# Loading a matmul's first B chunks in column halves and A by row tile, with two pairs of matmuls kept back behind each second transpose

## Chip, cores, metric

One core of one Trainium2 chip. The metric is device microseconds of the whole launch.

Besides the device time each run gives the span, from the core's first to its last instruction. I call the difference **the time outside the span**. Differences here are tenths of a microsecond in 1783, so I give the runs' spread and look for the same thing in the traces. The means of five runs are good to about 0.1 us. Kernels are compared only within the same rounds.

## The reference

```python
# a: 4096 x 4096, b: 4096 x 4096, float32; alpha = 0.01
x = np.matmul(a, b)
return np.where(x > 0, x, alpha * x)
```

## The kernel before

The output is computed in regions of 512 rows by 1024 columns: eight PSUM banks of 128 x 512, for row tile `mt` 0 to 3 and column half `nt` 0 or 1. Inputs are rounded to bf16. From the second stage on, loads round on the way, and VectorE transposes A. The first stage (1024 of K, in eight chunks) is hand-made to get TensorE (PE) going early: float32 loads on SyncE's queue, rounding on VectorE and ScalarE, and transposes of A on PE with an identity. A's part comes in two runs of 512 of K, for B's chunks 0 to 3 and 4 to 7. All is issued in one order list:

```python
order = [("b", 0), ("a", 0, 0, 1), ("a", 1, 0, 1), ("a", 2, 0, 1), ("a", 3, 0, 1)]
order += [("b", 1), ("b", 2), ("a", 0, 1, 2), ("b", 3), ("a", 2, 1, 1), ("a", 3, 1, 1)]
order += [("b", c) for c in range(4, KC)]
# ("b", chunk)   ("a", first tile, run of 512 of K, number of tiles)
for what, i, *more in order:
    if what == "a":
        ...
        nc.sync.dma_start(a_in[:, i:i + tiles, k], src)
    elif i:                                   # chunk 0 comes on ScalarE's queue
        nc.sync.dma_start(b_in[i], b_rows(pairs[0], 0, i))       # 512 KB
...
def turn_a(i, r, tiles):
    ...                                       # 4 PE transposes a tile, into bank ps7 for run 1
    if r and not shared:                      # tiles 0 and 1 of run 1: the copy out is held
        leaving.append(lambda: nc.vector.tensor_copy(to, turned))
    elif r:
        nc.vector.tensor_copy(to, turned)     # tiles 2 and 3
    else:
        nc.scalar.copy(to, turned)

def round_b(i):
    for nt, copy in ((0, nc.scalar.copy), (1, nc.vector.tensor_copy)):
        copy(b0[:, i, columns(nt)], b_in[i][:, columns(nt)])
    for leave in leaving:                     # the held copy follows the next chunk's cast
        leave()
    leaving.clear()
...
def work(keep=0):                             # emit all ready (mt, chunk) pairs but the last keep
    now = waiting[:len(waiting) - keep]
    ...
```

Bank `ps7` serves the transposes and is also the accumulator of tile 3's right half, the **late bank**. That accumulator can start only when the second copy out of the transposes is done.

## Time and profile before

| | before |
|---|---|
| device time, median of the first six runs | 1783.43 us (1783.37 to 1783.80) |
| span of the trace | 1781.684 us |
| time outside the span | 1.79 us |
| PE's first matmul of chunk 1 | 9.73 us |
| PE restarts with the late bank, the **restart** | 16.11 us |
| last matmul starts | 1778.289 us |
| transfers on SyncE's input queue / built instructions of VectorE | 14 / 311 |

The page and the timeline are in the prediction. The way to read them: PE is busy 99% of the span, so the only question is where its few idle tenths lie. They lie before the restart. After it PE has work without a break, save 0.15 us.

### The profile page before, as it was taken

The numbers are of one execution on the slowest core, as the hardware profiler recorded it, in microseconds if no ns is written. First come the engines' busy times: TensorE is split into PE (matmuls) and PEld (weight loads), VectorE is DVE, ScalarE is ACT, GpSimd is POOL, SyncE is SP. The second block draws the span as 40 slices with busy tenths as digits, with TensorE's granted clock in tenths as the row PEclk, the third lists the DMA queues.
The fourth block names the chain that finished last, engine by engine and source line by source line (L and its number), as shares of the span: only waits on it lengthen the run. The fifth ranks groups of instructions, "written<-read, shape, count | busy, mean of one in ns | idle before, by whom it ended". The sixth has DMA issues, their size and how long they took to land.

```text
span 1781.7 us, 18049 instructions
## 1 busy us (share of the span) xinstructions
PE 1767.0 (99%) x8104; PEld 807.7 (45%) x8267; DVE 144.8 (8%) x123; ACT 152.5 (9%) x271; POOL 365.8 (21%) x667
## 2 busy tenths in 40 slices
PE   9999999999999999999999999999999999999999
PEld 4444444444444444444444444444444444444444
DVE  4530000032000000002200000000220000000000
ACT  2010000000000000000000000000000000000001
POOL 5630200433002020144201202014320110301000
PEclk9999999999999999999999999999999999999999
DMA  9995653987039174398704917449860481835511
GB/s 249 201 253 114 117 129 87 190 131 124 36 95 189 48 121 116 95 191 134 124 24 96 187 48 143 93 104 196 134 121 13 112 172 48 164 73 120 117 48 47
DMA packets 161548, 214.06 MB, mean 120 GB/s; under 512 B 41536, under 2 KB 90816, under 8 KB 161472
## 3 DMA queue, kind: packets, MB, share of 16 engines
q0 software_dynamic: 140608, 139.50, 49.2%
q10 hardware_dynamic: 18432, 67.12, 9.7%
q1 hardware_dynamic: 2432, 6.29, 0.9%
q8 instruction: 64, 1.05, 0.2%
q14 instruction: 12, 0.10, 0.0%
HBM read 285.21 MB, written 67.11 MB: 198 GB/s over the span
## 4 chain that ended last, share of the span: by engine, by line
PE 98%; DMA 1%; issue 1%; POOL 0%; ACT 0%; DVE 0%
PE ps L160 98%; DMA bt<-in_b_dram 1%; DMA b_in<-in_b_dram 1%; POOL bt L140 0%; DVE at L300 0%; ACT bt L306 0%; PE turned L291 0%; ACT o L453 0%
## 5 line engine op out<-in xcount | busy, mean ns | idle before, releaser
L160 PE MATMUL ps<-bt,at 128*128 128x512 bf16 x8061 | 1761.1, 378 | 9.6 <-DVE at L300 0.6
L160 PEld LDWEIGHTS <-at 128*128 128x128 bf16 x8224 | 804.2, 98 | 964.3 <-issue 1.8
L140 POOL DMA_DIRECT2D bt<-in_b_dram x408 | 217.2, 539 | 1085.9 <-PE ps L160 963.7
L438 ACT ACTIVATE o<-ps 128x512 f32<-128x512 f32 x239 | 130.2, 595 | 1518.1 <-PE ps L160 1443.3
L123 DVE STREAM_TRANSPOSE at<-a 128x1024 uint32<-128x1024 uint32 (+2 forms) x64 | 112.5, 1791 | 1153.7 <-DMA a<-in_a_dram 595.8
L117 POOL DMA_DIRECT2D a<-in_a_dram x252 | 147.9, 593 | 194.3 <-DVE at L123 132.6
L238 DVE TENSOR_TENSOR part<-ps,part 128x512 f32<-128x512 f32 x32 | 20.2, 685 | 25.6 <-PE ps L160 25.6
L241 ACT ACTIVATE o<-part 128x1024 f32<-128x1024 f32 x8 | 8.5, 1057 | 77.1 <-DVE part L238 64.6
L306 ACT CAST bt<-b_in 128x512 bf16<-128x512 f32 x8 | 4.9, 618 | 9.7 <-DMA b_in<-in_b_dram 9.7
L234 DVE COPY part<-ps 128x512 f32<-128x512 f32 x8 | 5.3, 681 | 4.2 <-PE ps L160 4.2
L236 ACT COPY part<-ps 128x512 f32<-128x512 f32 x8 | 4.4, 593 | 13.7 <-issue 8.1
L89 PE MATMUL wp<-w 128*128 128x512 bf16 x11 | 4.3, 569 | 1.2 <-DVE x L80 1.2
L306 DVE CAST bt<-b_in 128x512 bf16<-128x512 f32 x8 | 3.4, 425 | 4.7 <-DMA b_in<-in_b_dram 4.7
L291 PE MATMUL turned<-ident,a_rounded 128*128 128x128 bf16 x32 | 3.0, 222 | 0.7 <-DVE a_rounded L274 0.7
L274 DVE CAST a_rounded<-a_in 128x512 bf16<-128x512 f32 (+1 forms) x7 | 3.2, 468 | 5.7 <-DMA a_in<-in_a_dram 5.6
L291 PEld LDWEIGHTS <-a_rounded 128*128 128x128 bf16 x32 | 2.3, 114 | 2.7 <-DVE a_rounded L274 2.1
L89 PEld LDWEIGHTS <-w 128*128 128x128 bf16 x11 | 1.4, 136 | 3.6 <-issue 2.4
L359 POOL CAST x<-bt 128x1 f32<-128x1 bf16 x1 | 0.2, 183 | 12.1 <-ACT bt L306 12.1
L302 ACT COPY at<-turned 128x512 bf16<-128x512 bf16 x4 | 2.3, 586 | 0.7 <-PE turned L291 0.5
L86 ACT ACT_TABLE_LOAD x1 | 1.3, 1283 | 1.2 <-PEq L472 1.2
L453 ACT ACTIVATE o<-ps 128x256 f32<-128x256 f32 x2 | 0.8, 383 | 6.0 <-PE ps L160 6.0
L300 DVE COPY at<-turned 128x1024 bf16<-128x1024 bf16 x1 | 0.7, 692 | 0.8 <-PE turned L291 0.8
(10 smaller groups left out, 2.1 us busy)
## 6 DMA issues: line engine op xcount, KB each, us to landing
bt<-in_b_dram POOLq DMA_DIRECT2D x408, 256.0 KB, 7.8
out_dram<-o ACTq DMA_DIRECT2D x127, 512.0 KB, 3.1
a<-in_a_dram POOLq DMA_DIRECT2D x244, 128.0 KB, 5.2
b_in<-in_b_dram SPq DMA_DIRECT2D x7, 512.0 KB, 8.5
a_in<-in_a_dram SPq DMA_DIRECT2D x6, 256.0 KB, 5.2
b_in<-in_b_dram ACTq DMA_DIRECT2D x1, 512.0 KB, 4.7
a_in<-in_a_dram SPq DMA_DIRECT2D x1, 512.0 KB, 7.5
a<-in_a_dram POOLq DMA_DIRECT2D x8, 64.0 KB, 5.6
```

The lines of the kernel that those rows point to most:

```text
L89: nc.tensor.matmul(wp, w[:, :P], w, start=True, stop=True)
L117: nc.gpsimd.dma_start(to, src.rearrange("(g i) w -> i g w", i=32))
L123: nc.vector.transpose(dst.rearrange("p c m e -> p c (m e)").bitcast(U32) .rearrange("p c (g i) -> p g c i", i=32), held[0][:, 4 * t0:4 * t ...
L140: nc.gpsimd.dma_start(new_b(pi, u)[:, c, :], b_rows(n, u, c))
L160: nc.tensor.matmul(ps, plain(t)[:, c, rows] if (mb, h, u) == (0, 0, 0) else t[:, c // 2, rows, c % 2], bt[pi, u][:, c, cols or slice(nt * ...
L234: nc.vector.tensor_copy(kept, banks[mt, nt])
L236: nc.scalar.copy(kept, banks[mt, nt])
L238: nc.vector.tensor_add(kept, banks[mt, nt], kept)
L241: nc.scalar.activation(o, part[h][:, mt, :], LRELU, alpha=alpha)
L291: nc.tensor.transpose(turned[:, c, slot, :], cols[:, i + t, c, :], ident)
L306: copy(b0[:, i, columns(nt)], b_in[i][:, columns(nt)])
L438: nc.scalar.activation(o[:, cols], banks[mt, nt], LRELU, alpha=alpha)
```

## The change

The intent: left halves of a chunk can be rounded before right ones have landed; A's second run can be transposed tile by tile; and more ready matmuls stand behind each second transpose, to cover the copy out. The core of the diff (renamings left out):

```diff
-    order += [("b", 1), ("b", 2), ("a", 0, 1, 2), ("b", 3), ("a", 2, 1, 1), ("a", 3, 1, 1)]
+    order += [("b", 1), ("b", 2), ("a", 0, 1), ("a", 1, 1), ("b", 3), ("a", 2, 1), ("a", 3, 1)]
...
-            nc.sync.dma_start(b_in[i], b_rows(pairs[0], 0, i))
+            for nt in range(NP):
+                nc.sync.dma_start(b_in[i][:, columns(nt)], b_rows(pairs[0], 0, i)[:, columns(nt)])
...
-        if r and not shared:
-            leaving.append(lambda: nc.vector.tensor_copy(to, turned))
-        elif r:
-            nc.vector.tensor_copy(to, turned)
-        else:
-            nc.scalar.copy(to, turned)
+        if slot == tiles - 1:
+            copy = nc.vector.tensor_copy if r else nc.scalar.copy
+            copy(to, turned[r].rearrange("p c t m -> p c (t m)"))
...
-        return next(m for m in range(len(order) - n) if order[n + 1 + m][0] == "b")
+        return next(m for m in range(KC) if order[n + 1 + m][0] == "b" or not order[n + 1 + m][2])
...
-            work(ahead(n) if r else 0)
+            work(ahead(n) + 1 if r and ahead(n) else 0)
...
-                work(max(1, ahead(n)))
+                work(ahead(n) + 1)
```

More of the change, by code (lines that the diff above doesn't have):

```diff
@@ L250 @@
     a_in = bt_pool.tile([P, MT, KW], FP32, name="a_in", tag="bt")
-    order = [("b", 0), ("a", 0, 0, 1), ("a", 1, 0, 1), ("a", 2, 0, 1), ("a", 3, 0, 1)]
-    order += [("b", 1), ("b", 2), ("a", 0, 1, 2), ("b", 3), ("a", 2, 1, 1), ("a", 3, 1, 1)]
+    order = [("b", 0), ("a", 0, 0), ("a", 1, 0), ("a", 2, 0), ("a", 3, 0)]
+    order += [("b", 1), ("b", 2), ("a", 0, 1), ("a", 1, 1), ("b", 3), ("a", 2, 1), ("a", 3, 1)]
     order += [("b", c) for c in range(4, KC)]
@@ L256, in columns, with run @@
         return slice(nt * NT, (nt + 1) * NT)
+    def run(r):
+        return slice(r * rw, (r + 1) * rw)
     for what, i, *more in order:
         if what == "a":
-            r, tiles = more
-            k = slice(r * rw, (r + 1) * rw)
-            src = a[i * P:(i + tiles) * P, k].rearrange("(t p) k -> p t k", p=P)
-            nc.sync.dma_start(a_in[:, i:i + tiles, k], src)
+            r = more[0]
+            nc.sync.dma_start(a_in[:, i, run(r)], a[i * P:(i + 1) * P, run(r)])
         elif i:
-            nc.sync.dma_start(b_in[i], b_rows(pairs[0], 0, i))
+            for nt in range(NP):
+                nc.sync.dma_start(b_in[i][:, columns(nt)], b_rows(pairs[0], 0, i)[:, columns(nt)])
@@ L266 @@
     a0 = new_a(0, 0, 0)
     b0 = new_b(0, 0)
-    leaving = []
-    both = []
-    def round_a(i, r, tiles):
-        k = slice(r * rw, (r + 1) * rw)
-        nc.vector.tensor_copy(a_rounded[:, i:i + tiles, k], a_in[:, i:i + tiles, k])
-    def turn_a(i, r, tiles):
-        k = slice(r * rw, (r + 1) * rw)
-        shared = r and tiles == 1
-        if shared and i == MT - 1:
-            turned = both.pop()
-        else:
-            tag = "ps7" if r else f"ps{4 + i}"
-            turned = psum_pool.tile([P, per, 2 if r else 1, P], BF16, name="turned", tag=tag)
-        if shared and i < MT - 1:
-            both.append(turned)
-        cols = a_rounded[:, :, k].rearrange("m t (p c) -> m t c p", c=per)
-        for t in range(tiles):
-            slot = i - (MT - 2) if shared else t
-            for c in range(per):
-                nc.tensor.transpose(turned[:, c, slot, :], cols[:, i + t, c, :], ident)
-        if both:
-            return
-        first = MT - 2 if shared else i
-        to = plain(a0)[:, r * per:(r + 1) * per, first * P:(i + tiles) * P]
-        turned = turned.rearrange("p c t m -> p c (t m)")
-        if r and not shared:
-            leaving.append(lambda: nc.vector.tensor_copy(to, turned))
-        elif r:
-            nc.vector.tensor_copy(to, turned)
-        else:
-            nc.scalar.copy(to, turned)
@@ new lines, with round_a, turn_a @@
+    turned = {}
+    def round_a(i, r):
+        nc.vector.tensor_copy(a_rounded[:, i, run(r)], a_in[:, i, run(r)])
+    def turn_a(i, r):
+        tiles = 2 if r else 1
+        slot = i % tiles
+        if slot == 0:
+            tag = "ps7" if r else f"ps{4 + i}"
+            turned[r] = psum_pool.tile([P, per, tiles, P], BF16, name="turned", tag=tag)
+        cols = a_rounded[:, i, run(r)].rearrange("m (p c) -> m c p", c=per)
+        for c in range(per):
+            nc.tensor.transpose(turned[r][:, c, slot, :], cols[:, c, :], ident)
+        if slot == tiles - 1:
+            to = plain(a0)[:, r * per:(r + 1) * per, (i - slot) * P:(i + 1) * P]
+            copy = nc.vector.tensor_copy if r else nc.scalar.copy
+            copy(to, turned[r].rearrange("p c t m -> p c (t m)"))
@@ L306, in round_b @@
             copy(b0[:, i, columns(nt)], b_in[i][:, columns(nt)])
-        for leave in leaving:
-            leave()
-        leaving.clear()
     there = {"a": [], "b": []}
@@ L342 @@
         if what == "a":
-            r, tiles = more
+            r = more[0]
             if n > 1:
-                round_a(i, r, tiles)
-            turn_a(i, r, tiles)
-            work(ahead(n) if r else 0)
-            there["a"] += [(i + t, r) for t in range(tiles)]
-            waiting += [(i + t, c) for t in range(tiles) for c in there["b"] if c // per == r]
+                round_a(i, r)
+            turn_a(i, r)
+            work(ahead(n) + 1 if r and ahead(n) else 0)
+            there["a"].append((i, r))
+            waiting += [(i, c) for c in there["b"] if c // per == r]
         else:
```

## The prediction

> **What bounds the kernel now.** I read the page first, then the PE timeline of the first 25 us, then the other engines' timeline there, then the chain of waits.
>
> ```profile
> span 1781.7 us, 18049 instructions
> ...
> PE 1767.0 (99%) x8104; PEld 807.7 (45%) x8267; DVE 144.8 (8%) x123; ACT 152.5 (9%) x271; POOL 365.8 (21%) x667
> ...
> L160 PE MATMUL ps<-bt,at 128*128 128x512 bf16 x8061 | 1761.1, 378 | 9.6 <-DVE at L300 0.6
> ```
>
> TensorE is the bound. In the trace single 128x512 matmuls start 0.2157 us apart; 8192 of them are worth 1767.0 us, the busy time on the page (the 378 ns is a pipelined latency, and 131 records are missing). So 99% of the span is work that the change does not touch. Going through the starts of all PE records, I find after 16.11 us one gap that is no missing record: 0.15 us at 23.9, where the second region's first bank waits for its copy out. Everything to be won lies before 16.11 us. The PE timeline there (start, length with the last one's latency, count, idle time before):
>
> ```profile
> 8.40 0.60 PE L160 MATMUL ps<-bt,at 128*128 128x512 bf16 x2
> 9.22 3.48 PE L160 MATMUL ps<-bt,at 128*128 128x512 bf16 x14 [0.22 <-ACT at L302]
> 12.54 0.61 PE L291 MATMUL turned<-ident,a_rounded 128*128 128x128 bf16 x8
> 13.35 1.02 PE L160 MATMUL ps<-bt,at 128*128 128x512 bf16 x4 [0.20 <-ACT bt L306]
> 14.26 0.41 PE L291 MATMUL turned<-ident,a_rounded 128*128 128x128 bf16 x4
> 14.51 0.59 PE L160 MATMUL ps<-bt,at 128*128 128x512 bf16 x2
> 14.95 0.39 PE L291 MATMUL turned<-ident,a_rounded 128*128 128x128 bf16 x4
> 15.17 0.38 PE L160 MATMUL ps<-bt,at 128*128 128x512 bf16 x1
> 16.11 9.16 PE L160 MATMUL ps<-bt,at 128*128 128x512 bf16 x40 [0.57 <-DVE at L300]
> ```
>
> I count idle in issue slots, since the shown idle subtracts a latency: 0.2157 for a matmul, 0.056 for a transpose. Before 11.2 us there are waits that the change leaves alone. From the eight transposes on there are three: for the cast of B chunk 3 about 0.15 us (12.98 plus one unrecorded matmul is 13.20; it goes on at 13.35), for the cast of A tile 2 (14.21 to 14.26 and a 0.03 slower first transpose) 0.08, and for the copy out of the last transpose, 15.17+0.216=15.384 to 16.113, 0.73. Sum 0.96 us. The copy matters because the late accumulator (row tile 3, right half) lives in the bank that the transposes use.
>
> The others in that stretch (L306 casts B, L274 casts A, L298 and L300 copy transposes out):
>
> ```profile
> 10.04 0.43 DVE L306 CAST bt<-b_in 128x512 bf16<-128x512 f32 x1 [0.87 <-DMA b_in<-in_b_dram]
> 11.47 0.69 DVE L274 CAST a_rounded<-a_in 128x1024 bf16<-128x1024 f32 x1 [0.99 <-DMA a_in<-in_a_dram]
> 12.67 0.62 ACT L306 CAST bt<-b_in 128x512 bf16<-128x512 f32 x1 [2.01 <-DMA b_in<-in_b_dram]
> 12.68 0.43 DVE L306 CAST bt<-b_in 128x512 bf16<-128x512 f32 x1 [0.52 <-DMA b_in<-in_b_dram]
> 13.18 0.69 DVE L298 COPY at<-turned 128x1024 bf16<-128x1024 bf16 x1
> 13.79 0.79 DVE L274 CAST a_rounded<-a_in 128x512 bf16<-128x512 f32 x2
> 15.37 0.69 DVE L300 COPY at<-turned 128x1024 bf16<-128x1024 bf16 x1 [0.79 <-PE turned L291]
> ```
>
> Before, VectorE casts chunk 3 first and copies transposes after. The chain of waits names the same pieces:
>
> ```profile
> 5.49 7.16 DMA b_in<-in_b_dram
> ...
> 12.67 0.63 ACT bt L306
> ...
> 15.37 0.70 DVE at L300
> ...
> 16.11 7.50 PE ps L160 x34
> ```
>
> [...] the casts of B on ScalarE and VectorE wait behind earlier copies that are not ready. My result hangs on this order. [...] Halves have rows of 2 KB where whole chunks have 4 KB. The trace gives a 2 KB packet 85 to 88 ns and a 4 KB one 159 to 167, so the finer form costs some 5%. [...] chunk 7 took 1.83 us (17.84 to 19.67) against 1.28 of its neighbours, once the software queue's packets had begun at 17.57.
>
> **The change part by part.** The order of both built programs shows: the same 64 matmuls and 32 transposes in the first part, the same from the late bank on; the last chunks alone come in another size.
>
> *Halves.* Landings before: A tiles 5.29, 6.12, 6.79, 7.45, chunks 1 and 2 8.72 and 10.02, A's second run 11.37, chunk 3 12.65, last two A tiles 13.33 and 13.99. A 256 KB piece of 2 KB rows takes 0.667 (the A tiles: 0.67, 0.66, 0.68, 0.66). From 7.45 on the pieces land at 8.12, 8.79 (chunk 1), 9.45, 10.12 (chunk 2), 10.79, 11.45 (A 0, 1), 12.12, 12.79 (chunk 3), 13.45, 14.12 (A 2, 3). Left halves come 0.55 earlier, all else 0.1 later. Chunk 1's left half gains nothing: ScalarE is at its copies until 9.06.
>
> *Second run by tile.* The casts become 10.81 to 11.24 and 11.48 to 11.90, 0.43 each: ready before PE wants them.
>
> *Order.* PE is unchanged up to 11.24. Then two matmuls (11.24, 11.456), four transposes 11.67 to 11.895, two matmuls, four transposes 12.33 to 12.55, three matmuls, chunk 3's left one: no wait until 13.41. But there is a new order on VectorE: the copy out is no longer held behind chunk 3's cast, it comes ahead. It starts 0.257 after the start of the last transpose (12.926 to 13.183 before), so 12.495+0.257=12.75, and ends 13.44. Queued work overlaps by 0.08, so chunk 3's right half (landed 12.79) is cast 13.36 to 13.78, and PE resumes 0.052 later at 13.835: **0.42 idle**. A tile 2 (landed 13.45) is cast 13.70 to 14.125; the matmul's slot ends 14.05, the transposes start 14.18: **0.13**, with 0.03 for the first. They end 14.43; two matmuls to 14.86; tile 3 (cast by 14.57) is turned 14.86 to 15.09. Copy: 15.03+0.257=15.29, +0.692=15.98, PE at 16.03. Meanwhile three matmuls are kept back instead of one, to 15.73: **0.30**. Sum 0.88 us against 0.96: 16.03 against 16.113, **0.08 us gained**. Hiding the second copy wins 0.43, and most goes to the first copy that now stands ahead of the cast.
>
> *After it.* From 16.03 the same work follows. The rest shifts with PE as long as operands are there: chunk 7 is wanted right-half at 22.9, estimated there by 20.7 with its cast; the next A pieces come by the software queue, some 0.5 us earlier, since their start hangs on chunk 3's left cast. The next stage's B lands over 4 us ahead. So 1783.37-0.08=1783.29.
>
> **The rivals.** (a) *The transfers become the bound.* At most eight are in flight (issue waits on the eighth before it), now half as large: 8 x 0.667=5.3 us of work against a shortest time to landing of 4.5 us at the start. I see no bubble, but slack for tile 2 is only 0.22 us. With 0.72 a piece tile 2 lands at 13.93, PE restarts about 16.28: 1783.55; a 0.5 us bubble makes 1783.9. For it: 23 transfers instead of 15. Against: A tiles of the very same size follow one another without a hole. (b) *The intent comes true*: all 0.96 us filled, 1782.4. For it: more PE work behind each transpose. Against: VectorE's order, worked out above. If the cast slipped ahead of the copy, I would expect 1782.9. (c) *Hidden anyway*: gain or loss is taken up by a later wait, 1783.37. Against: no later wait but the 0.15 us, which moves along.
>
> **Range and chances.** One mechanism sets the sum, with errors of 0.05 us a step; runs spread 0.07. Below, half of (b) gives 1782.85; above, (a) with a small bubble 1783.85. So 1783.29, range 1782.85 to 1783.85. Two per cent is 36 us, over thirty times all the idle in reach: same 0.99.
>
> **What would show it.** Right: VectorE's copy before the cast of chunk 3's right half, which starts near 13.36; PE gaps near 13.4 (0.42), 14.1 (0.13), 15.7 (0.30); the late bank at 16.03; queue 1 with 3456 packets (2432 plus 896 rows plus 128 for eight transfers more). Wrong: A tile 2 or chunk 3 landing over 0.3 us after my times (rival a), no gap at 13.4 (b), or a new wait after 16 us (c).

What it uses of the hardware the traces show. In that of before, matmul starts are 0.2157 us apart and transpose starts 0.056. Packets of 2 KB take 84 ns and those of 4 KB 161, the medians up to 20 us. Of the order on VectorE: the right half of chunk 4 had landed at 15.29, and VectorE was idle from 14.58 to 15.37, yet the cast began only at 15.98, behind the copy that became ready at 15.37. For ScalarE the trace of after shows it: the left half of chunk 1 landed at 8.06 and was cast from 9.00 on, behind a copy that began at 8.51 after an idle of 0.24. Of the eight transfers in flight: the ninth issue began at 5.49, chunk 0 had landed at 5.47. Why chunk 7 took 1.83 us is not shown, only that the software queue's packets had begun by then.

## The result, and the profile after

| | before | after |
|---|---|---|
| device time, median of six runs each | 1783.43 us (1783.37 to 1783.80) | **1784.26 us** (1784.04 to 1784.47) |
| span of the trace | 1781.684 | 1781.913 |
| time outside the span | 1.79 | **2.13** |
| first matmul of chunk 1 | 9.732 | 9.668 |
| restart | 16.113 | **16.351** |
| last matmul starts | 1778.289 | 1778.513 |

The ratio is 1.0004, interval 0.9991 to 1.0017: the same within 2%, but by some 0.8 us slower, and above my range. A ratio is the mean time of one kernel's fast runs over that of the other's of the same rounds, so not quite the ratio of the medians. The two groups of six do not overlap.

From the page of after:

```profile
span 1781.9 us, 18060 instructions
...
PE 1767.8 (99%) x8104; PEld 806.7 (45%) x8267; DVE 145.0 (8%) x124; ACT 152.3 (9%) x271; POOL 365.6 (21%) x667
...
q1 hardware_dynamic: 3456, 6.29, 1.0%
```

The 3456 packets are those predicted. The PE timeline of after in the stretch that the prediction showed of before:

```profile
12.03 0.60 PE L160 MATMUL ps<-bt,at 128*128 128x512 bf16 x2
12.47 0.41 PE L284 MATMUL turned<-ident,a_rounded 128*128 128x128 bf16 x4
12.94 0.81 PE L160 MATMUL ps<-bt,at 128*128 128x512 bf16 x3
14.00 0.38 PE L160 MATMUL ps<-bt,at 128*128 128x512 bf16 x1 [0.25 <-DVE bt L292]
14.47 0.42 PE L284 MATMUL turned<-ident,a_rounded 128*128 128x128 bf16 x4
14.72 0.59 PE L160 MATMUL ps<-bt,at 128*128 128x512 bf16 x2
15.16 0.41 PE L284 MATMUL turned<-ident,a_rounded 128*128 128x128 bf16 x4
15.41 4.77 PE L160 MATMUL ps<-bt,at 128*128 128x512 bf16 x20
```

The last line hides a gap (lines merge): the chain of waits of after has the copy and the restart.

```profile
15.61 0.70 DVE at L288
16.31 0.04 issue
16.35 7.28 PE ps L160 x33
```

And VectorE:

```profile
12.92 0.69 DVE L288 COPY at<-turned 128x1024 bf16<-128x1024 bf16 x1 [0.51 <-PE turned L284]
13.53 0.42 DVE L292 CAST bt<-b_in 128x512 bf16<-128x512 f32 x1
13.99 0.43 DVE L273 CAST a_rounded<-a_in 128x512 bf16<-128x512 f32 x1
14.67 0.43 DVE L273 CAST a_rounded<-a_in 128x512 bf16<-128x512 f32 x1 [0.26 <-DMA a_in<-in_a_dram]
```

The copy does stand ahead of chunk 3's right cast. Counted in issue slots from the single starts, PE's idle from chunk 1 on is 0.20 us before tile 0's transposes, 0.03 before tile 1's, 0.42 for the right cast, 0.28 before tile 2's, 0.03 before tile 3's, 0.30 for the second copy: 1.25 us against 0.96. The 0.42 and the 0.30 are the prediction's. The rest is new. It comes of late landings, which I read from the trace's completion counters (us). Counted from chunk 0's, which ScalarE issues, the right half of chunk 2 is the **ninth transfer**; its late landing is called the **stall** below.

| transfer | before | predicted | after | a second trace of after |
|---|---|---|---|---|
| chunk 2, left half | | 9.45 | 9.38 | 9.38 |
| chunk 2, right half (before: whole) | 10.02 | 10.12 | **10.61** | 10.06 |
| A tile 0 | (pair, 11.37) | 10.79 | 11.27 | 10.72 |
| A tile 1 | 11.37 | 11.45 | 11.96 | 11.40 |
| chunk 3, right half (before: whole) | 12.65 | 12.79 | 13.29 | 12.75 |
| A tiles 2, 3 | 13.33, 13.99 | 13.45, 14.12 | 13.96, 14.65 | 13.43, 14.11 |

The right half of chunk 2 came 1.23 us after its left half, not 0.67, and all behind it stayed late. The windows view (PE, weight loads, DVE, ACT, POOL, then clock, DMA share, GB/s) for one microsecond, before:

```profile
8.50:9.50 1.00, 0.78 (x4) 0.12 (x3) 0.43 (x1) 0.92 (x2) 0.00 (x0) 1.00 0.99 393
```

and after:

```profile
8.50:9.50 1.00, 0.78 (x3) 0.11 (x2) 0.43 (x1) 0.99 (x2) 0.00 (x0) 1.00 1.02 305
```

The DMA engines count as busy, but move 305 GB/s instead of 393. Some packets took 0.33 to 0.88 us where 0.085 is usual. A transfer's counter goes up in 16 steps, and it has landed with the last step. The steps of the right half of chunk 2 came between 9.48 and 10.61, a spread of 1.13 us against 0.56 for the transfer before.

So three questions: are the slow packets chance, or the change's doing? Is the predicted order on VectorE what costs time? And where do 0.34 us outside the span come from?

### The profile page after: what moved, and what is told of

It is laid out like the page before. It is cut to its first block, busy times and chain, and to the rows that moved or that the text cites. A ratio compares the mean times of both kernels' runs of the same rounds, so it can differ in the third digit from the quotient of the medians.

```text
span 1781.9 us, 18060 instructions
## 1 busy us (share of the span) xinstructions
PE 1767.8 (99%) x8104; PEld 806.7 (45%) x8267; DVE 145.0 (8%) x124; ACT 152.3 (9%) x271; POOL 365.6 (21%) x667
## 3 DMA queue, kind: packets, MB, share of 16 engines
q1 hardware_dynamic: 3456, 6.29, 1.0%
## 4 chain that ended last, share of the span: by engine, by line
PE 98%; DMA 1%; issue 0%; SPq 0%; DVE 0%; ACT 0%
PE ps L160 98%; DMA a_in<-in_a_dram 0%; DMA b_in<-in_b_dram 0%; SPq L264 0%; DVE at L288 0%; PE turned L284 0%; DVE a_rounded L273 0%; ACT o L435 0%
```

## The experiments

To compare traces, I take the restart less the start of chunk 1's first matmul, since the very first landings shift from execution to execution (chunk 1's first matmul starts between 9.53 and 10.00 us in the traces). It is 6.38 before (6.38 to 6.44 in four padded copies of it), 6.68 after; my prediction amounts to 16.03-9.73=6.30. "Slow" is the sum, over the packets of SyncE's input queue between 6.5 and 17 us that took over 60 ns longer than usual, of what they took too long; usual is about 0.085 us for 2 KB and 0.16 for 4 KB, and the sums are good to some 5%. It is spread over 16 engines.

**The changed kernel again.** No edit.

> The changed kernel once more, unaltered, for a second trace. Restart means here the start of the late bank's first matmul after the second copy out of the transposes: 16.11 us in the trace of before, 16.35 in that of after. Theory S (the slow packets of the ninth transfer, the right half of chunk 2, which landed 0.56 us late, come of the small transfers): the same transfer lands 10.4 to 10.7 again, more than 1.0 us after the left half, restart 16.2 to 16.5, time 0.6 to 0.9 us over before. Theory A (an accident of that one execution): it lands 0.67 us after the left half, near 10.05 to 10.12, and PE restarts near 16.03. On the time outside the span (device time less span: 1.79 us before, 2.13 after): if it belongs to the build it is 2.1 again.

Measured: 1784.03 us (1783.67 to 1784.13; before in the same call 1783.58). In its trace the ninth transfer landed on time. PE, by the timeline:

```profile
12.46 1.03 PE L160 MATMUL ps<-bt,at 128*128 128x512 bf16 x4
13.74 0.38 PE L160 MATMUL ps<-bt,at 128*128 128x512 bf16 x1 [0.25 <-DVE bt L292]
14.11 0.41 PE L284 MATMUL turned<-ident,a_rounded 128*128 128x128 bf16 x4
14.36 0.59 PE L160 MATMUL ps<-bt,at 128*128 128x512 bf16 x2
14.79 0.39 PE L284 MATMUL turned<-ident,a_rounded 128*128 128x128 bf16 x4
15.02 5.21 PE L160 MATMUL ps<-bt,at 128*128 128x512 bf16 x22
```

This is the predicted schedule: gaps of 0.42, 0.19 (with the slower first transpose) and 0.30, restart 15.96, 6.32 after chunk 1's start. The span is 1781.528, 0.16 less than before's trace. Yet the device time of this execution is 1783.67, since the time outside the span is again 2.14. So the stall comes and goes, and the 0.34 us outside belong to the build.

**Whole chunks, the rest of the change kept.**

```diff
-            for nt in range(NP):
-                nc.sync.dma_start(b_in[i][:, columns(nt)], b_rows(pairs[0], 0, i)[:, columns(nt)])
+            nc.sync.dma_start(b_in[i], b_rows(pairs[0], 0, i))
```

> The changed kernel with B in whole chunks of 512 KB; A's second run by tile, the copy ahead of the cast and the kept pairs stay. Theory S: no stall; A tiles 0 and 1 land near 10.7 and 11.37, chunk 3 12.65, last A tiles 13.33 and 13.99. By my slot count PE then waits 0.15 for chunk 3's left cast, 0.27 for the right one behind the copy, 0.13 for A tile 2, 0.30 for the second copy: restart 16.03, 0.08 before that of before. Time 0.0 to 0.2 us under before if the time outside the span is that of before, 0.2 to 0.4 over it if it is 2.1. Theory A: the same, so this run tells S from A only together with the run of halves alone. Rival: the order on VectorE is the whole loss, then restart stays at 16.3 and the time 0.6 to 0.9 over.

Measured: 1783.91 us (1783.65 to 1784.16). Gaps 0.16, 0.26, 0.15 and 0.30, restart 15.97 (6.29), last matmul 1778.145, 0.14 earlier than before; slow 0.1 us; outside 1.79. Span though 1781.964: from the last matmul's start to the span's end (the **tail**) it took 3.82 us against 3.40. The trace's semaphore records show why. At the end SyncE waits for its completion counters one after another, some 0.06 us each (0.059 to 0.064 in the trace of before, from 1779.47 to 1779.83). Transfers use eight counters in turn. With one transfer more, the last one falls on a counter that is waited for early, and eight waits follow its landing instead of one. So this 0.42 us is an accident of counting. Without it the mean span is 1782.10-0.42=1781.68, 0.09 under before's in the same call (1781.77), which is no more than such means are good to.

**Halves only, in the kernel before.** The same lines the other way round:

```diff
-            nc.sync.dma_start(b_in[i], b_rows(pairs[0], 0, i))
+            for nt in range(NP):
+                nc.sync.dma_start(b_in[i][:, columns(nt)], b_rows(pairs[0], 0, i)[:, columns(nt)])
```

> The kernel before with B in halves and nothing else changed. Theory S: the right half of chunk 2, still the ninth transfer, lands about 0.5 us late, and with it all behind: the A pair near 11.9, transposes near 12.7, chunk 3 near 13.3, A tile 2 near 14.0; with the cast ahead of the copy on VectorE the tile's cast starts near 14.26, PE restarts 16.5 to 16.6, time 0.4 to 0.9 us over before. Theory A: no stall, landings as I had predicted, restart 16.1 to 16.2, time within 0.15 of before plus what lies outside the span.

Measured: 1784.09 us (1783.96 to 1784.14). No stall in this trace (slow 0.35 us), restart 16.37 (6.45), the 0.73 us gap as before; outside 2.13, and two waits at the end instead of one. Halves alone bring nothing, and they carry the time outside.

**The first copy held behind chunk 3's cast, in the changed kernel.**

```diff
-            copy(to, turned[r].rearrange("p c t m -> p c (t m)"))
+            src = turned[r].rearrange("p c t m -> p c (t m)")
+            if r and i < MT - 1:
+                leaving.append(lambda: copy(to, src))
+            else:
+                copy(to, src)
```

with the flush at the end of the rounding of a chunk, as before.

> The changed kernel with the first copy out held behind chunk 3's cast on VectorE, as in the kernel before. My prediction's 0.42 us gap for the right half (13.37 to 14.00 in the trace of after) should go. With the late landings of theory S: the cast of the right half 13.3 to 13.73, PE gap before it 0.2; the copy ends 14.34, A tile 2 is cast 14.26 to 14.68, so the gap moves to that tile's transposes, restart 16.4 to 16.6, time 0.0 to 0.25 over the changed kernel. Without a stall restart 15.95. If it were the order that costs the time, it would come out 0.3 to 0.4 us faster than the changed kernel.

Measured: 1784.13 us (1783.96 to 1784.30). Here the ninth transfer was 0.34 us late (slow 2.2). The gap before the right cast shrank to 0.23, but the one before tile 2's transposes grew to 0.76, restart 16.54 (6.76). So which of the two stands first decides only where VectorE's chain of copy, cast, cast makes PE wait. The order is not the loss seen in after, and undoing it did not help in these five runs. Without a stall it was expected to be worth 0.08 us (15.95 against 16.03); no trace without one shows it.

**Kept pairs only, in the kernel before.**

```diff
-            work(ahead(n) if r else 0)
+            work(2 * ahead(n) if r else 0)
```

> The kernel before with only the kept pairs: after the transposes of A tile 2 no matmul runs, tile 3 is transposed at once, and all three ready matmuls stand behind it while the second copy goes on. Worked out from the trace of before: tile 3 is cast by 14.58, its transposes 14.63 to 14.86, copy 15.06 to 15.75, PE restarts at 15.80 instead of 16.11, an idle of 0.12 before tile 3 and 0.30 after the three matmuls in place of the 0.73. Nothing else changes, so the last matmul comes 0.31 us earlier and the time is 1783.2 to 1783.3 against 1783.57. Rival: the 0.73 us are taken back by the 0.15 us wait at 23.9 or a later one: no change.

Measured: **1783.30 us** (1783.15 to 1783.54) against 1783.51 (1783.27 to 1783.75) of before. PE:

```profile
13.44 1.02 PE L160 MATMUL ps<-bt,at 128*128 128x512 bf16 x4 [0.19 <-ACT bt L306]
14.37 0.79 PE L291 MATMUL turned<-ident,a_rounded 128*128 128x128 bf16 x8
14.99 5.21 PE L160 MATMUL ps<-bt,at 128*128 128x512 bf16 x22
```

Tile 3 is transposed right after tile 2, three matmuls stand behind it, and the gap for the second copy is 0.30 instead of 0.73. Restart 6.10 after chunk 1's start, against 6.38: 0.28 us won, 0.31 expected. The mean span fell by 0.22 (1781.54 against 1781.76). It is the fastest of all kernels here. Of the parts tried alone this one expression is the only one that won anything. A's transposes tile by tile were never tried alone.

**Halves from chunk 3 on, chunks 1 and 2 whole, in the changed kernel.**

```diff
-            for nt in range(NP):
-                nc.sync.dma_start(b_in[i][:, columns(nt)], b_rows(pairs[0], 0, i)[:, columns(nt)])
+            pieces = 1 if i < 3 else NP
+            for n in range(pieces):
+                cols = slice(n * RN // pieces, (n + 1) * RN // pieces)
+                nc.sync.dma_start(b_in[i][:, cols], b_rows(pairs[0], 0, i)[:, cols])
```

> The changed kernel with chunks 1 and 2 whole and halves only from chunk 3 on. The ninth transfer (A tile 1) then has 5.3 us between its issue and its turn instead of 4.0. Theory L (the late landing comes of that short lead: 3.97 and 3.98 us in the two traces with slow packets, 4.02 and 4.04 in the two without): no transfer lands more than 0.72 us after the one before it up to 17 us, restart 15.95 to 16.05, last matmul 0.05 to 0.2 us before that of before. Accident theory: slow packets as often as with all halves. Time outside the span: 20 input transfers on SyncE's queue, 14 before and 22 in the changed kernel; 1.79 if there is a step above 20, 2.05 if linear, 2.13 if the step is below. The last transfer falls on another of the eight completion counters, with three waits behind its landing instead of one: 0.12 us longer tail.

Measured: 1783.91 us (1783.76 to 1784.18). No transfer late, restart 6.36, outside 2.15, tail 0.11 longer. Slow packets: five, 0.6 us in sum, at 9.1 to 9.4. The mean span less the tail's 0.11 is 1781.67, again 0.09 under before's, though this trace's 6.36 shows only 0.02 won at the restart. The last matmul came later than expected (1778.518), because that execution started 0.27 us late: its chunk 1 began at 10.00.

**Chunk 1 in quarters, in the changed kernel.**

The same edit, with `pieces = 2 * NP if i == 1 else NP`.

> The changed kernel with chunk 1 in four quarters, so that the ninth transfer (its last quarter) gets a lead of about 3.0 us instead of 4.0. Theory L: it lands 0.8 to 1.2 us late in every execution and all behind it with it, PE restarts at 16.6 to 17.0, last matmul 0.4 to 0.9 us after that of the changed kernel, time 1784.6 to 1785.2. Accident theory: landings within 0.1 us of those of the run without slow packets plus 0.05, restart about 16.0, time as the changed kernel, plus 0.37 us in the tail for the counter that the last transfer falls on, in both theories.

Measured: 1784.73 us (1784.33 to 1784.82). Restart 16.63 (6.87), slow 6.8 us, the most of any variant of the change. But not as expected: the ninth transfer itself was only 0.05 us late; the tenth lost 0.16 and A tile 1 another 0.46. With this lead of 3.1 us packets were slow, then, but no sharp bound showed at which one transfer fails. The tail was 0.36 longer, as foreseen, and the time outside the span was 1.78, with even more transfers.

**Eight tiny loads more, in the kernel before.**

```diff
+    scratch = small_pool.tile([P, 8, 8], FP32, name="scratch")
+    for j in range(8):
+        nc.sync.dma_start(scratch[:, j, :], b[:P, 8 * j:8 * j + 8])
```

> The kernel before with eight tiny loads more (4 KB each, into a scratch tile nobody reads) at the end of SyncE's input queue, as many more transfers as the changed kernel has and the same last counter. Inside the span nothing should change: restart near 16.1, last matmul near 1778.3. If the 0.34 us outside the span belong to the number of SyncE's transfers or instructions: device time less span 2.13, time 1783.9. If they belong to the halves themselves: 1.79, time 1783.57.

Measured: 1783.54 us (1783.26 to 1783.72), before 1783.51; outside 1.81. So the number of transfers does not set the time outside the span.

**One fill more on VectorE, in the changed kernel.** What the builds with 2.13 share is the length of VectorE's instruction stream:

```diff
+        if r == 4:
+            idle = small_pool.tile([P, 8], FP32, name="idle")
+            for _ in range(1):
+                nc.vector.memset(idle, 0.0)
```

> The changed kernel with one small fill of an unread scratch tile on VectorE, in mid-run where VectorE is idle. The 0.34 us outside the span go with no count of transfers (the kernel before with eight more: 1.81; the quarters with ten more: 1.78). What the ten traces share is the length of VectorE's instruction stream: 309 records and 313 have 1.78 to 1.81, 311 and 312 have 2.13 to 2.15. If it is that stream, 313 here give 1.79 outside the span and a time 0.35 us under the changed kernel, 1783.6 to 1783.9. If it is not: 2.13 again and 1784.0 to 1784.3.

Measured: **1783.63 us** (1783.27 to 1783.78), before 1783.52; outside 1.82 in the trace and 1.75 to 1.80 in the other runs. One useless instruction made the changed kernel some 0.35 us faster. Its trace has the stall again: ninth transfer 0.49 us late, slow 4.9, restart 16.40 (6.65). This shows the two losses apart.

**Three fills, in the kernel before**, to show it the other way round.

> The kernel before with three such fills on VectorE, so that its stream has the 312 records of the changed kernel; everything else is untouched. If the stream's length sets the time outside the span: 2.13 instead of 1.79, time 1783.85 to 1783.95 with a span as before. If not: 1.79 and 1783.5.

Measured: 1783.57 us, outside 1.78. Inconclusive: the fills took the place of three wait instructions, and the stream kept its 311 built instructions. With a scratch column for each fill it grew, once by three and once by four:

```diff
+        if r == 4:
+            idle = small_pool.tile([P, 3, 8], FP32, name="idle")      # or 4 instead of 3
+            for j in range(3):
+                nc.vector.memset(idle[:, j, :], 0.0)
```

> The earlier try with three fills did not do what it should: the fills took the place of three separate wait instructions, and VectorE's stream kept its 311 built instructions (309 records). Here the three fills have a place each, and the built stream has 314 instructions, as many as the changed kernel; everything else is that of before. If that length sets the time outside the span: 2.13 instead of 1.79 us, time 1783.85 to 1783.95. If not: 1.79 and 1783.5.

> The same with four fills, 315 built instructions on VectorE, as many as the changed kernel with one fill had, which gave 1.79 outside the span. If the place in the stream counts and not its length as such: 1.79 again and 1783.5, one instruction more being 0.34 us faster than the run with three fills. If each instruction costs: above 2.13.

Measured, with before at 1783.52 in both:

| VectorE's built instructions | kernel | device time, us | outside the span, us |
|---|---|---|---|
| 311 | before | 1783.52 | 1.79 |
| 314 | before, three fills | 1783.90 (1783.66 to 1784.25) | 2.15 |
| 315 | before, four fills | 1783.62 (1783.45 to 1783.80) | 1.78 |

All builds fit: 311 and 315 instructions have 1.78 to 1.82 (eight builds), 313 and 314 have 2.13 to 2.15 (six). From 314 to 315 instructions on an engine that has nothing to do at the end, the time outside the span fell by 0.37 us in the kernel before (2.15 to 1.78) and by 0.31 in the changed kernel (2.13 to 1.82). 312 was not tried, so no rule is shown, only that these counts differ. Which part of the launch takes the time, the traces do not tell: it lies before their first or after their last instruction.

**A short lead with whole chunks.** This one tells whether halves as such make packets slow. In the kernel before, A tiles 1 to 3 of the first run come in two pieces each:

```diff
+            pieces = 2 if r == 0 and i else 1
+            for j in range(pieces):
+                k = slice(r * rw + j * rw // pieces, r * rw + (j + 1) * rw // pieces)
```

(The two lines that make and issue the transfer move into the loop.) The built program has eight completion counters for chunk 0's transfer and SyncE's. So the ninth issue waits for chunk 0 to land (5.47, then 5.49 in the trace of before; 5.38, then 5.40 in that of after) and came between 5.25 and 5.72 us in all traces, whatever the size of the others. With small pieces ahead of it, its turn comes sooner.

> The kernel before, B in whole chunks, but A tiles 1 to 3 of the first run in two pieces each. The ninth transfer is now chunk 1, whole, with some 2.0 us between its issue and its turn (5.9 in the kernel before for its ninth, 4.0 in the changed kernel, 3.1 in the quarters). If a short lead makes packets slow whatever the transfer's form: packets of B over 60 ns above their usual time between 7 and 11 us, 1 us or more of them in sum over the 16 engines (0 to 0.4 in the four traces with whole chunks), chunk 1 landing 0.15 us or more after 8.85, PE's restart and the last matmul later than in the kernel before. If it is the halves of B with their 2 KB rows: no such packets, chunk 1 at 8.7 to 8.85. VectorE has 314 built instructions here, so 2.13 us outside the span if that counts; the last counter gives some 0.2 to 0.3 us more of tail.

Measured: 1786.18 us (1785.76 to 1787.92), before 1783.52; ratio 1.0017, interval 1.0002 to 1.0032. Chunk 1, whole, landed at 11.07 instead of 8.7, the steps of its counter spread from 8.45 to 11.07. The slowest packets, up to 1.4 us each, are of 4 KB, so of whole chunks. PE waits:

```profile
9.21 0.39 PE L160 MATMUL ps<-bt,at 128*128 128x512 bf16 x1 [0.16 <-ACT at L305]
11.76 4.65 PE L160 MATMUL ps<-bt,at 128*128 128x512 bf16 x13 [2.16 <-ACT bt L309]
```

This traced execution is the slowest of the four: after PE's gap of 2.3 us (9.43 to 11.76) its granted clock was 0.5 from 12.44 to 15.86 us, with matmuls 0.427 us apart instead of 0.2157, which costs some 1.7 us (half of 3.4, an estimate). The others took 1.7 us or more less, at a granted clock of 1.0. What brought the half clock in this one no run shows.

| | lead of the ninth, us | slow, us | ninth late by, us |
|---|---|---|---|
| before and five kernels with the same transfers ahead of the ninth | 5.8 to 5.9 | 0 to 0.1 | 0 |
| changed, chunks 1 and 2 whole | 5.3 | 0.6 | 0 |
| changed, whole chunks | 5.2 | 0.1 | 0 |
| before, halves | 4.0 | 0.4 | 0 |
| changed kernel, three traces | 4.0, 4.0, 4.0 | 4.5, 0.7, 4.9 | 0.56, 0.01, 0.49 |
| changed, cast first | 4.0 | 2.2 | 0.34 |
| changed, quarters | 3.1 | 6.8 | 0.05, with the next ones 0.67 |
| before, A in pieces, whole chunks | 2.1 | 16.5 | 2.3 |

The lead is the time from the ninth's issue to the landing of the eighth. With 2.1 us whole chunks have slow packets too (16.5 us), so they came here without halves of B. That halves add nothing of their own is not shown: near 5.2 us they have 0.6 us of slow packets and whole chunks 0.1. Nor was the lead ever shortened but by smaller transfers ahead. At 4 us, the changed kernel's, it goes either way from one execution to the next. What a slow packet waits for no run shows.

## Why the prediction was wrong

**The schedule on PE and VectorE: right.** The copy ahead of the cast, gaps of 0.42 and 0.30 at the second and fourth wait, and a net gain of 0.08: the traces without a stall give 6.32 for the changed kernel and 6.29 and 6.36 for two variants, for the predicted 6.30. Those two variants have mean spans 0.09 under before, once the tail's waits are taken off. A gain this small the times can't confirm. The main statement, that 0.43 won at the second copy is given back at the first, holds.

**"I see no bubble": wrong.** This is the first step that failed. I compared eight transfers' work (8 x 0.667=5.3 us) with a shortest time to landing of 4.5 us at the start and called the rest slack. The count was wrong: the ninth issue waits for chunk 0, and by then (5.38) A tile 0 had landed as well (5.22). So six pieces stood ahead of it, 6 x 0.667=4.0 us, the lead that the traces show, and 4.7 us with its own: 0.2 us of slack and not 0.8. Nor is 4.5 us a limit: the ninth landed 5.2 us after its issue in the two traces with the stall, 4.7 in the one without, and 3.5 as a quarter. In two of three traces of the changed schedule the lead was not enough, and the stall cost 0.36 and 0.33 us at the restart (6.68 and 6.65 less the 6.32 of the third). Why a packet is slow stays open. Rival (a) was the right one. I gave it 0.5 us for a bubble, and bubbles of 0.49 and 0.56 came; its consequence for PE was smaller than I wrote, since part of it went into waits that were there anyway. Over all 15 runs of this schedule the mean span is about 0.2 us above before's instead of 0.08 below (six runs +0.39, where before's span is its time less 1.79; five +0.07; four with the fill +0.07). The late landings therefore cost some 0.3 us on the average, an estimate from these figures: it takes in whatever the first landings shifted, and the three groups ran in different calls.

**"After it. From 16.03 the same work follows": wrong by 0.34 us.** I took everything outside the span for a constant. Three more instructions on VectorE made it 2.13 instead of 1.79. This is the steadier term: with one instruction more the changed kernel measures 1783.63.

The sum of it: -0.08 predicted, +0.34 outside the span, and +0.47 for late landings in the first six runs or +0.15 in the next five give +0.73 or +0.41. Measured were +0.8 and +0.45 by medians. The sum closes because the last term is what the spans leave over; only the 0.34, and the 0.36 and 0.33 of the two traces, are measured by themselves. Neither of the two terms alone would have left the range (1783.29 plus 0.34 or 0.47). My base was low as well: 1783.37 and the spread of 0.07 came from three runs, where six had a median of 1783.43 and a spread of 0.43.

**Rivals (b) and (c).** The intent did not come true, for the reason given. But part of it came true: the kept pairs alone, without the copy's new place, won 0.28 us at the restart. I had the working for this at hand and did not split the change in the prediction. Nothing was hidden later (c): every shift of the restart reached the last matmul.

## What to carry to other kernels

When transfers are cut finer and a fixed number may be under way (eight here), work out the lead of the first transfer that must wait for a slot: from its issue to its turn. It shrank here from 5.9 to 4.0 us, and that cost some 0.3 us on the average by the estimate above, more than the 0.08 that the schedule was to gain. When a change is worth tenths of a microsecond, compare span and time outside it, and the tail after the last matmul, before explaining anything: one instruction more on an idle engine and one transfer in the count of eight moved 0.37 and 0.42 us here. And try each part of a change alone: the kept pairs had the lowest median of all, 0.2 us under before.
